# One-core hybrid decoder layer on Trainium2: low parts of expert 1's gate weights on VectorE, slot words fixed later, row tiles of one expert kept in the 64-slot tiles

## The chip, the core and the metric

The kernel runs on one core of one Trainium2 chip. The metric is the device time of one execution in microseconds, as the median of several runs. The profiles come from one execution each; times in them count from the start of the span.

The engines are called TensorE (PE in the profile, its weight loads PEld), VectorE (DVE), ScalarE (ACT), GpSimd (POOL) and SyncE (SP). In this kernel SP issues the loads of weights and of the row tables; GpSimd issues all gathers and scatters that go by an index.

## What is computed

One decoder layer on 2048 tokens of width 1024 with 16 learned meta tokens ahead of them: a pooling mixer and a gated linear attention side by side, an output projection, a routed mixture of 16 small SwiGLU experts, and a last norm. The part that matters here is the mixture:

```python
def hier_moe(x, w_rg, b_rg, w_re, b_re, w_gate, w_up, w_down):
    # g_logits, e_logits: x times two small matrices, plus biases
    g_prob = jax.nn.softmax(g_logits, axis=-1)
    g_sel = jnp.argmax(g_logits, axis=-1)                    # one of 4 groups
    e_prob = jax.nn.softmax(e_logits, axis=-1)               # of the 4 experts of that group
    top_p, top_i = lax.top_k(e_prob, TOP_K_IN_GROUP)         # the best two
    top_p = top_p / jnp.sum(top_p, axis=-1, keepdims=True)
    weights = p_g * top_p
    for e in range(N_EXPERTS):
        h = jax.nn.silu(xt @ w_gate[e]) * (xt @ w_up[e])     # 1024 -> 256
        y = y + combine[:, e:e + 1] * (h @ w_down[e])        # 256 -> 1024
```

Each token so has two experts of one group. Everything is float32.

## The kernel before, in words

**Split products.** A float32 product is made of three TensorE matmuls on rounded halves: high by high, low by high, high by low. `split` (L109 to L112) makes the halves of a tile: ScalarE writes the high part (L111), and VectorE, or the engine that is handed in, subtracts it from the tile for the low part (L112). `split_scaled` (L107, L108) does the same with a scale, for token rows that come out of a transpose.

**Slots.** The program does not compute all experts on all tokens. Routing gives each (token, expert) pair a slot, and each expert works on its slots: three row tiles j = 0, 1, 2 of 128, 128 and 64 slots (`rows`), 320 in all, for the experts at the first ten places, and two tiles (256 slots) for the places from `LARGE` = 10 on. Experts 0 and 1 have fixed places; the other fourteen are ranked by their token counts in `rank_experts` (L708), and `expert_at` then tells which expert's weights and table rows a place takes. Below, "expert e" means the one at place e.

**Routing, tile by tile.** Sixteen tiles of 128 tokens go through `out_proj`, `route_pick` (L579: logits, best group, best two experts, A = the two picks of each token as zeros and ones) and `route_rest` (L619). In `route_rest` TensorE multiplies A with a triangular matrix (`before_b`, L645) and the sum of all earlier tiles' A with ones (L647); the result says how many tokens ahead of each have the same expert, and VectorE makes slot numbers of it (L662 to L676) and a row of words for each pair (`rec`). GpSimd scatters these rows to a table in DRAM (L690), two scatters a tile. For the last tile (`t == NT`) two more matmuls make the total counts (L641, L642), which stand ahead of the picks, and VectorE adds them (L643); `rank_experts` reads them.

**Row tables and words.** `load_places` (L1105) reads the table back by SP: places 0 and 1 in one load, then 14 loads for a place each. A row has the token number (word 0, for the gather of its tokens), the weight (word 3), and others; words 1 and 2 say where a finished row is scattered or gathered, and `fix_words` (L1107 to L1121, seven VectorE instructions) works them out for a range of places.

**Around the end of routing.** Experts 0 and 1 start on the tokens of the early tiles before routing has ended: their tiles 0 and 2 are gathered early, and `gate_rows` (L984; matmuls L995 to L997) runs their gate and up products with the tokens as the stationary side, one accumulator for each tile. Tile 1 of each, the late rows, follows when the table is complete (`first_rows`). The order of these steps on an engine is that of the program, moved by the scheduler and by `must_follow`, which puts one instruction behind others on its engine: the last picks follow step k = 2 of the third group of `gate_rows` (`gate_ops[2]`, L1138).

**Weights.** Weight chunks of 128 x 1024 come in the order of `stream`: 0 to 3 expert 0's gate and up chunks, 4 to 7 expert 1's, 8 and 9 expert 0's down chunks, and so on. `load_chunks` (L747, issue L759) puts each in a tile of the pool `raw` of three buffers; `split_chunk` (L767) makes its halves. Expert 1's four chunks take their low parts from GpSimd (L1140); each frees a `raw` buffer, and SP then issues the load of the next chunk. SP works in order.

**The expert loop.** For expert e, `gate_up` (L963; matmuls L975 to L977; for experts 0 and 1 `gate_rows`) makes the hidden rows; `down` (L1020) multiplies them with the down weights (L1036 to L1041), and ScalarE evacuates the result with the slot's weight (L1052) into the expert's row tiles `RT[e]`. The rows are added to those of the token's other expert by indexed adds between `oe` and the row tile (L924); when e + 1 is under way, `square`, `finish` and `scale_out` (L1072, L1078) norm them and GpSimd scatters them to the output (L924, `out_dram`). Between the matmuls of `gate_up`, the function `between` puts the next expert's transposes (L946), weight splits and weight loads. The tiles of the tokens are `XG` (of the pool `xg`, and the two 64-slot tiles xs0 and xs1, `short`, in turn for j = 2). Row tiles `RT[e]` come from a pool `xr` of `RB` = 6 buffers, taken in turn (L1024), so one waits until the rows in its buffer have been scattered to the output.

Of the kernel before, what the change touches and what calls it, by code (L numbers as in the profile page):

```python
# [12 lines left out]
OP = mybir.AluOpType  # L13
# [4 lines left out]
NT = 16  # L18
# [8 lines left out]
LARGE = 10  # L27
# [43 lines left out]
def body(ctx, tc, I, O):  # L71
    nc = tc.nc
    V = nc.vector
# [82 lines left out]
    iota16 = iota("iota16", 16, 1)  # L156
    FIXED = 2
# [15 lines left out]
    counts = sl.tile([128, 16], F32, name="counts")  # L173
    place = per.tile([128, 16], F32, name="place")
# [445 lines left out]
    def route_rest(t):  # L620
# [9 lines left out]
        if t == EARLY + 1:  # L630
            nc.tensor.matmul(pp[:, 1], ones_b, acc[i % 2], start=True, stop=True)
            early = pp[:, 1]
            V.tensor_copy(counts, early)
            for row, at in ((late1, 128.0), (late2, float(SMALL)), (late3, float(CAP))):
                V.tensor_scalar(row[:, FIXED:], early[:, FIXED:], -1.0, at, op0=OP.mult, op1=OP.add)
            V.tensor_scalar(late2[:, :FIXED], early[:, :FIXED], -1.0, float(CAP), op0=OP.mult, op1=OP.add)
            V.tensor_scalar(late2[:, :FIXED], late2[:, :FIXED], 128.0, None, op0=OP.min)
            V.tensor_copy(late3[:, :FIXED], late2[:, :FIXED])
            V.scalar_tensor_tensor(late0[:, FIXED:], early[:, FIXED:], 48.0, iota16[:, FIXED:], op0=OP.mult, op1=OP.add)
        elif t == NT:  # L640
            nc.tensor.matmul(pp[:, 1], ones_b, acc[i % 2], start=True, stop=False)  # L641
            nc.tensor.matmul(pp[:, 1], ones_b, A, start=False, stop=True)  # L642
            V.tensor_tensor(counts, pp[:, 1], counts, op=OP.add)  # L643
        pp = pp[:, 0]
        picked[0] = nc.tensor.matmul(pp, before_b, A, start=True, stop=(t == EARLY + 1))  # L645
        if t != EARLY + 1:
            nc.tensor.matmul(pp, ones_b, acc[i % 2], start=False, stop=True)  # L647
        ngm, eg, sg, nm1, p2, den, w = T("ngm", 1), T("eg", 4), T("sg", 1), T("nm1", 1), T("p2", 1), T("den", 1), T("w", 2)
        V.tensor_scalar(ngm, gm, -1.0, None, op0=OP.mult)
        nc.scalar.activation(eg, lg[:, 0:4], AF.Exp, bias=ngm, accum_out=sg)  # L650
# [253 lines left out]
    with ExitStack() as c2:  # L904
# [30 lines left out]
        def row_tile(own=False):  # L935
            return mk.tile([128, D], F32, name="xr", bufs=RB) if own else me.tile([128, D], F32, name="xg", bufs=GB - 2)
# [83 lines left out]
        def down(e, js=None):  # L1020
            js = js or JS[e]
            ahead = e >= NE - 2
            if e not in RT:
                RT[e] = [row_tile(True) for j in JS[e]]  # L1024
            tags = ("sp", "o", "ds", "tp", "zg", "m2") if e else ("mm", "mm", "ds", "m2", "ds", "m2")
            units = [(j, a, bank(tags[2 * j + a])) for j in js for a in range(2)]

# [107 lines left out]
            for k in range(KB):  # L1135
                transposes(0, k, (0, 2), added[0])
        early = [gate_rows(0, 0, "mm"), gate_rows(0, 2, "mm", lambda k: k < 6 or transposes(1, k - 6, (0, 2)))]
        must_follow(picked[0], [gate_ops[2]])  # L1138
        for k in range(4):
            split_chunk(nc.gpsimd)  # L1140
            load_chunks(min(8 + k, 10))
        for k in range(2, KB):
            transposes(1, k, (0, 2))
        load_places(0, FIXED, slice(0, FIXED))
        fix_words(0, FIXED, iota16)
        for e in range(FIXED, NE):
            load_places(e, e + 1, expert(e))
        first_rows = [ind(XG[e][1], hn_dram, col(e, 1, 0), False) for e in range(2)]
# [16 lines left out]
                    transposes(0, i, (1,))  # L1165

        early_1 = [gate_rows(1, 0, "sp"), gate_rows(1, 2, "o", early_rest)]
        down(0, (0, 2))
        for e in range(NE):
            def between(i):  # L1170
                if e + 1 < NE and i % 2 == 0:
                    for k in range(i, i + 2):
                        transposes(e + 1, k, None if e else (1,))
                if e == 0:
                    if i in (2, 6):
                        fix_words(*((2, 9) if i == 2 else (9, 16)), place)
                    if i == 0:
                        for op in load_chunks(10 + WRB, mk):
                            must_follow(op, first_rows)
# [170 lines left out]
```

## Time and profile before

| | |
|---|---|
| median of the runs (1121.91, 1123.40, 1123.54) | 1123.4 us |
| the profiled execution, its span | 1121.29 us, 1119.5 us |
| mean granted clock of TensorE | 0.982 |
| TensorE (PE) busy | 1055.8 us, 94% |
| TensorE weight loads (PEld) | 946.5 us, 85% |
| VectorE (DVE) | 779.8 us, 70% |
| ScalarE (ACT) | 565.7 us, 51% |
| GpSimd (POOL) | 313.8 us, 28% |

A row of a timeline gives the start in the span, the duration, engine, line, operation, output and inputs, and in brackets how long the engine had been idle and what ended that. A row of the waits gives an engine, its instruction and whom it waited for: the total, how often, and the longest. A row of the windows gives each engine's busy time in a stretch, the granted clock of TensorE as a share of full speed (its levels are 1.2 and 2.4 GHz), and how busy the DMA engines were.

### The profile page before, as it was taken

The numbers are of one execution on the slowest core, as the hardware profiler recorded it, in microseconds if no ns is written. First come the engines' busy times: TensorE is split into PE (matmuls) and PEld (weight loads), VectorE is DVE, ScalarE is ACT, GpSimd is POOL, SyncE is SP. The second block draws the span as 40 slices with busy tenths as digits, with TensorE's granted clock in tenths as the row PEclk, the third lists the DMA queues.
The fourth block names the chain that finished last, engine by engine and source line by source line (L and its number), as shares of the span: only waits on it lengthen the run. The fifth ranks groups of instructions, "written<-read, shape, count | busy, mean of one in ns | idle before, by whom it ended". The sixth has DMA issues, their size and how long they took to land. (4 is left out here: it accounts for less than half of the span.)

```text
span 1119.5 us, 19115 instructions
## 1 busy us (share of the span) xinstructions
PE 1055.8 (94%) x6614; PEld 946.5 (85%) x6614; DVE 779.8 (70%) x2649; ACT 565.7 (51%) x1192; POOL 313.8 (28%) x276
## 2 busy tenths in 40 slices
PE   7999999999999999999999998879999999989982
PEld 5888888888888889999999998558998899988861
DVE  6476666545555776878777788747787788867873
ACT  7545444334433643333333334337767777667741
POOL 2000000000000000121111105524677777776551
PEclk9999999999999999999999999989999999989996
DMA  8412332111121352533434344488888997889852
GB/s 279 166 66 76 107 101 90 62 57 48 67 85 57 115 196 67 170 142 120 145 124 151 114 153 160 132 235 237 221 248 230 242 264 214 231 256 311 255 152 74
DMA packets 64471, 174.09 MB, mean 156 GB/s; under 512 B 21012, under 2 KB 21317, under 8 KB 64368
## 3 DMA queue, kind: packets, MB, share of 16 engines
q1 hardware_dynamic: 36272, 105.72, 27.7%
q0 software_dynamic: 25504, 58.53, 20.0%
q10 hardware_dynamic: 2592, 8.55, 2.1%
q8 instruction: 54, 0.88, 0.3%
q14 instruction: 49, 0.40, 0.1%
HBM read 143.74 MB, written 57.74 MB: 180 GB/s over the span
## 5 line engine op out<-in xcount | busy, mean ns | idle before, releaser
L441 POOL DMA_DIRECT2D y_dram<-y x16 | 8.6, 541 | 391.2 <-DVE y L439 391.2
L924 POOL DMA_INDIRECT oe<-xr,tab x40 | 69.3, 1732 | 69.0 <-ACT xr L1052 57.3
L321 PE MATMUL mm<-wb,XL 128*128 128x512 f32 (+1 forms) x240 | 83.6, 348 | 0.0
L322 PE MATMUL mm<-wb,XH 128*128 128x512 f32 (+1 forms) x240 | 83.0, 346 | 0.0
L690 POOL DMA_INDIRECT table<-rec,ix x32 | 33.3, 1042 | 176.8 <-DVE tmp L703 85.4
L320 PE MATMUL mm<-wb,XH 128*128 128x512 f32 (+1 forms) x240 | 82.2, 342 | 0.0
L924 POOL DMA_INDIRECT xr<-oe,tab x39 | 75.4, 1932 | 17.8 <-issue 9.8
L523 PE MATMUL mm<-XL,ws 128*128 128x256 f32 (+1 forms) x256 | 73.0, 285 | 0.2 <-DVE XL L112 0.2
L522 PE MATMUL mm<-XH,ws 128*128 128x256 f32 (+1 forms) x256 | 73.0, 286 | 0.0
L524 PE MATMUL mm<-XH,ws 128*128 128x256 f32 (+1 forms) x256 | 72.2, 282 | 0.0
L111 ACT ACTIVATE XH<-xt 128x1024 fp32r<-128x1024 f32 x32 | 33.8, 1058 | 56.4 <-PE mm L524 36.0
L924 POOL DMA_INDIRECT out_dram<-xr,tab x39 | 55.6, 1426 | 20.8 <-DVE sr_y L60 7.4
L975 PE MATMUL mm<-xh,ws 128*128 128x320 f32 (+1 forms) x168 | 51.3, 306 | 0.0
L976 PE MATMUL mm<-xl,ws 128*128 128x320 f32 (+1 forms) x168 | 51.2, 305 | 0.0
L977 PE MATMUL mm<-xh,ws 128*128 128x320 f32 (+1 forms) x168 | 51.0, 304 | 0.0
L320 PE MATMUL mm<-ws,XH 128*128 128x512 f32 x112 | 47.4, 423 | 2.0 <-ACT XH L111 2.0
L321 PEld LDWEIGHTS mm<-wb,XL 128*128 128x128 f32 x240 | 45.4, 189 | 4.4
L1078 DVE SCALAR_TENSOR_TENSOR xr<-xr,sr_y,fw 128x1024 f32<-128x1024 f32 (+1 forms) x39 | 48.7, 1278 | 0.5
L320 PEld LDWEIGHTS mm<-wb,XH 128*128 128x128 f32 x240 | 45.1, 188 | 4.6
L322 PEld LDWEIGHTS mm<-wb,XH 128*128 128x128 f32 x240 | 45.1, 188 | 4.5
L523 PEld LDWEIGHTS mm<-XL,ws 128*128 128x128 f32 x256 | 48.1, 188 | 0.7 <-DVE XL L112 0.4
L524 PEld LDWEIGHTS mm<-XH,ws 128*128 128x128 f32 x256 | 48.4, 189 | 0.3 <-issue 0.2
(654 smaller groups left out, 3840.8 us busy)
## 6 DMA issues: line engine op xcount, KB each, us to landing
raw<-in_wgu_e_dram SPq DMA_DIRECT2D x42, 512.0 KB, 5.2
xt<-in_xT_dram SPq DMA_DIRECT2D x32, 512.0 KB, 3.5
xn<-in_xn_dram SPq DMA_DIRECT2D x32, 512.0 KB, 3.5
wr<-in_wgu_e_dram SPq DMA_DIRECT2D x22, 512.0 KB, 5.9
raw<-in_wd_e_dram SPq DMA_DIRECT2D x20, 512.0 KB, 5.6
hn_dram<-xn ACTq DMA_DIRECT2D x16, 512.0 KB, 3.3
oe<-xn POOLq DMA_DIRECT2D x16, 512.0 KB, 3.7
wr<-in_wd_e_dram SPq DMA_DIRECT2D x12, 512.0 KB, 5.8
```

Of the source, the lines that this page charges most:

```text
L111: return (nc.scalar.activation(hi, src, AF.Copy), (eng or V).tensor_tensor(lo, src, hi.bitcast(F32), op=OP.subtract))
L320: nc.tensor.matmul(q, xh[:, k, :], wh[:, c0:c1_], start=(k == 0), stop=False)
L321: nc.tensor.matmul(q, xl[:, k, :], wh[:, c0:c1_], start=False, stop=False)
L322: nc.tensor.matmul(q, xh[:, k, :], wl[:, c0:c1_], start=False, stop=(k == KB - 1))
L522: nc.tensor.matmul(ps[:, b], WS[k][0][:, c], XH[:, k, o:], start=(k == 0), stop=False)
L523: nc.tensor.matmul(ps[:, b], WS[k][0][:, c], XL[:, k, o:], start=False, stop=False)
L524: nc.tensor.matmul(ps[:, b], WS[k][1][:, c], XH[:, k, o:], start=False, stop=(k == KB - 1))
L924: return nc.gpsimd.indirect_dma_start(out=out_, out_offset=off if scatter else None, in_=in_, in_offset=None if scatter else off, bounds_c ...
L975: nc.tensor.matmul(p[:, c0:c1_], wh, xh, start=(k == 0), stop=False)
L976: nc.tensor.matmul(p[:, c0:c1_], wh, xl, start=False, stop=False)
L977: nc.tensor.matmul(p[:, c0:c1_], wl, xh, start=False, stop=(k == KB - 1))
L1078: V.scalar_tensor_tensor(x[:n], x[:n], r[:n], fw[:n], op0=OP.mult, op1=OP.mult)
```

## The change

It has six edits.

1. In `route_rest` of the last tile the two matmuls of the totals, and VectorE's addition, stand behind the two matmuls of the picks instead of ahead of them.
2. The last picks follow step k = 6 of that group of `gate_rows` instead of step 2.
3. The low parts of expert 1's four weight chunks are made by VectorE instead of GpSimd; they follow `routed`, the last tile's cast of slot numbers.
4. `fix_words` for places 0 and 1 stands behind expert 1's early `gate_rows` instead of ahead of the 14 loads of single places.
5. `fix_words` for places 2 to 8 and 9 to 15 stand in expert 1's `between` instead of expert 0's.
6. Expert 10, the first with 256 slots, takes xs0 and xs1 as its row tiles instead of two of the pool `xr`. The buffers of the pool that it had (those of expert 8's tiles 0 and 1) go to expert 11, those of expert 11 to expert 12, and so on.

```diff
--- before.py
+++ after.py
@@ -637,14 +637,14 @@
             V.tensor_scalar(late2[:, :FIXED], late2[:, :FIXED], 128.0, None, op0=OP.min)
             V.tensor_copy(late3[:, :FIXED], late2[:, :FIXED])
             V.scalar_tensor_tensor(late0[:, FIXED:], early[:, FIXED:], 48.0, iota16[:, FIXED:], op0=OP.mult, op1=OP.add)
-        elif t == NT:
-            nc.tensor.matmul(pp[:, 1], ones_b, acc[i % 2], start=True, stop=False)
-            nc.tensor.matmul(pp[:, 1], ones_b, A, start=False, stop=True)
-            V.tensor_tensor(counts, pp[:, 1], counts, op=OP.add)
-        pp = pp[:, 0]
+        total, pp = pp[:, 1], pp[:, 0]
         picked[0] = nc.tensor.matmul(pp, before_b, A, start=True, stop=(t == EARLY + 1))
         if t != EARLY + 1:
             nc.tensor.matmul(pp, ones_b, acc[i % 2], start=False, stop=True)
+        if t == NT:
+            nc.tensor.matmul(total, ones_b, acc[i % 2], start=True, stop=False)
+            nc.tensor.matmul(total, ones_b, A, start=False, stop=True)
+            V.tensor_tensor(counts, total, counts, op=OP.add)
         ngm, eg, sg, nm1, p2, den, w = T("ngm", 1), T("eg", 4), T("sg", 1), T("nm1", 1), T("p2", 1), T("den", 1), T("w", 2)
         V.tensor_scalar(ngm, gm, -1.0, None, op0=OP.mult)
         nc.scalar.activation(eg, lg[:, 0:4], AF.Exp, bias=ngm, accum_out=sg)
@@ -1021,7 +1021,7 @@
             js = js or JS[e]
             ahead = e >= NE - 2
             if e not in RT:
-                RT[e] = [row_tile(True) for j in JS[e]]
+                RT[e] = short if e == LARGE else [row_tile(True) for j in JS[e]]
             tags = ("sp", "o", "ds", "tp", "zg", "m2") if e else ("mm", "mm", "ds", "m2", "ds", "m2")
             units = [(j, a, bank(tags[2 * j + a])) for j in js for a in range(2)]
 
@@ -1135,14 +1135,13 @@
             for k in range(KB):
                 transposes(0, k, (0, 2), added[0])
         early = [gate_rows(0, 0, "mm"), gate_rows(0, 2, "mm", lambda k: k < 6 or transposes(1, k - 6, (0, 2)))]
-        must_follow(picked[0], [gate_ops[2]])
+        must_follow(picked[0], [gate_ops[6]])
         for k in range(4):
-            split_chunk(nc.gpsimd)
+            must_follow(split_chunk()[1], [routed])
             load_chunks(min(8 + k, 10))
         for k in range(2, KB):
             transposes(1, k, (0, 2))
         load_places(0, FIXED, slice(0, FIXED))
-        fix_words(0, FIXED, iota16)
         for e in range(FIXED, NE):
             load_places(e, e + 1, expert(e))
         first_rows = [ind(XG[e][1], hn_dram, col(e, 1, 0), False) for e in range(2)]
@@ -1165,15 +1164,16 @@
                     transposes(0, i, (1,))
 
         early_1 = [gate_rows(1, 0, "sp"), gate_rows(1, 2, "o", early_rest)]
+        fix_words(0, FIXED, iota16)
         down(0, (0, 2))
         for e in range(NE):
             def between(i):
                 if e + 1 < NE and i % 2 == 0:
                     for k in range(i, i + 2):
                         transposes(e + 1, k, None if e else (1,))
+                if e == 1 and i in (2, 6):
+                    fix_words(*((2, 9) if i == 2 else (9, 16)), place)
                 if e == 0:
-                    if i in (2, 6):
-                        fix_words(*((2, 9) if i == 2 else (9, 16)), place)
                     if i == 0:
                         for op in load_chunks(10 + WRB, mk):
                             must_follow(op, first_rows)
```

The line numbers of the changed kernel are shifted a little: its picks are L641 and L643, its totals L645 and L646.

On TensorE, the last tile's picks and totals stood in expert 0's group of 64 rows in this way before (`mm` is the accumulator of `gate_rows`, `ws` and `xh`, `xl` its weights and tokens; `A` the picks, `acc` the sum of earlier tiles; the row with - is gone from this place):

```order
 L997 MATMUL mm<-ws_79,xh_8620 64x512
-L642 LDWEIGHTS ones_b
-L642 MATMUL m_8533<-A,ones_b 128x16
 L995 MATMUL mm<-ws_80,xh_8620 64x512
 L996 MATMUL mm<-ws_80,xl_8621 64x512
 L997 MATMUL mm<-ws_81,xh_8620 64x512
-L645 LDWEIGHTS before_b
-L645 MATMUL m_8533<-A,before_b 128x16
-L647 LDWEIGHTS ones_b
-L647 MATMUL m_8533<-acc_188,ones_b 128x16
 L995 MATMUL mm<-ws_80,xh_8620 64x512
```

and now in this way:

```order
 L997 MATMUL mm<-ws_85,xh_8620 64x512
+L641 LDWEIGHTS before_b
+L641 MATMUL m_8533<-A,before_b 128x16
+L643 LDWEIGHTS ones_b
+L643 MATMUL m_8533<-acc_188,ones_b 128x16
+L645 LDWEIGHTS ones_b
+L645 MATMUL m_8533<-acc_188,ones_b 128x16
+L646 LDWEIGHTS ones_b
+L646 MATMUL m_8533<-A,ones_b 128x16
 L946 MATMUL zg<-ident,xs_8627 128x128
```

The picks moved four steps further on, and the totals, which stood ahead of them and one of them in the first group of 128 rows, are now behind.

On VectorE, behind the last tile's routing, the changed kernel has this (`raw` and `wb` are a weight chunk and its halves, L722 to L725 the end of the ranking, `tp` and `zg` transposed tokens):

```order
L722 TENSOR_TENSOR sq<-sq,iota_114 128x196
L703 SCALAR_TENSOR_TENSOR tmp,sv_all<-E,lev 128x16
L112 TENSOR_TENSOR wb_87<-raw,wb_86 128x1024
L724 TENSOR_REDUCE t_8604<-sq 128x14
L112 TENSOR_TENSOR wb_89<-raw,wb_88 128x1024
L725 CAST expert_at<-t_8604 128x14
L112 TENSOR_TENSOR wb_91<-raw,wb_90 128x1024
L108 SCALAR_TENSOR_TENSOR wb_99<-tp,vecs,wb_98 128x192
L108 SCALAR_TENSOR_TENSOR wb_101<-zg,vecs,wb_100 128x192
```

Of expert 1's low parts the first three stand among the last steps of the ranking; the fourth follows a few rows on. Before, there was none of the four here.

The words of places 2 to 8 (L1115, 128x336) stood here on VectorE before (`HB` are the halves of hidden rows, `xl_8621` low halves of expert 0's tokens, eight of 128x128 for its late rows):

```order
L112 TENSOR_TENSOR HB<-zg,HB 128x2x128
L1004 TENSOR_TENSOR h<-mm,h 64x256
L112 TENSOR_TENSOR HB<-tp,HB 128x2x64
L1115 TENSOR_TENSOR sq<-tab,iota_114 128x336
L108 SCALAR_TENSOR_TENSOR xl_8621<-zg,vecs,xh_8620 128x128
L108 SCALAR_TENSOR_TENSOR xl_8621<-tp,vecs,xh_8620 128x128
L1116 TENSOR_TENSOR sq<-sq,place 128x336
```

and now here:

```order
L112 TENSOR_TENSOR HB<-zg,HB 128x2x128
L1004 TENSOR_TENSOR h<-mm,h 64x256
L108 SCALAR_TENSOR_TENSOR xl_8621<-zg,vecs,xh_8620 128x128
L112 TENSOR_TENSOR HB<-tp,HB 128x2x64
L108 SCALAR_TENSOR_TENSOR xl_8621<-zg,vecs,xh_8620 128x128
L108 SCALAR_TENSOR_TENSOR xl_8621<-tp,vecs,xh_8620 128x128
L1115 TENSOR_TENSOR sq<-tab,iota_114 128x336
L108 SCALAR_TENSOR_TENSOR xl_8621<-zg,vecs,xh_8620 128x128
L1116 TENSOR_TENSOR sq<-sq,place 128x336
```

They are behind three of the eight low halves, where they were ahead of all eight.

## Rows read from the trace of the kernel before

**Rows 1.** Windows: start:end, length; PE, PEld, DVE, ACT, POOL busy; clock, DMA share, GB/s.

```profile
695.00:744.80 49.80, 36.15 (x157) 24.55 (x156) 31.75 (x137) 17.66 (x38) 21.75 (x16) 0.86 0.54 167
709.70:713.20 3.50, 3.50 (x10) 1.85 (x9) 3.50 (x20) 0.74 (x2) 1.52 (x1) 0.51 0.02 5
735.30:740.30 5.00, 4.96 (x14) 3.27 (x15) 2.94 (x11) 1.66 (x5) 0.00 (x0) 0.50 0.64 201
982.10:1007.31 25.21, 21.25 (x138) 19.82 (x137) 16.54 (x34) 15.26 (x27) 17.37 (x13) 0.86 0.83 261
1007.31:1028.04 20.73, 19.64 (x143) 18.00 (x141) 18.21 (x36) 16.26 (x29) 14.15 (x8) 1.00 0.92 286
```

**Rows 2.** Waits from 695 to 745, those of TensorE.

```profile
PE zg L946 <- DVE xl L108: 7.0, 1, 7.0
...
PE m L641 <- DVE tmp L668: 2.7, 1, 2.7
PE m L642 <- DVE A L615: 2.7, 1, 2.7
```

**Rows 3.** Timeline of GpSimd, end of routing.

```profile
695.47 7.08 POOL L112 TENSOR_TENSOR wb<-raw,wb 128x1024 fp32r<-128x1024 f32 x3 [6.59 <-PE ds L572]
...
708.84 2.38 POOL L112 TENSOR_TENSOR wb<-raw,wb 128x1024 fp32r<-128x1024 f32 x1 [1.83 <-ACT wb L111]
714.03 1.03 POOL L690 DMA_INDIRECT table<-rec,ix  x1 [2.81 <-DVE sq L721]
715.36 1.76 POOL L690 DMA_INDIRECT table<-rec,ix  x1 [0.30 <-DVE t L724]
```

**Rows 4.** Timeline of VectorE, end of routing and the words of places 2 to 8.

```profile
696.61 1.32 DVE L663 TENSOR_TENSOR v<-v,late 128x16 f32<-128x16 f32 x1
...
700.23 2.35 DVE L667 TENSOR_TENSOR t<-lev,late_step 128x16 f32<-128x16 f32 x1
...
711.23 0.16 DVE L662 TENSOR_TENSOR v<-m,per_slot 128x16 f32<-128x16 f32 x1
...
713.58 0.16 DVE L676 CAST ix<-vv 128x2 int32<-128x2 f32 x1
...
715.04 1.22 DVE L112 TENSOR_TENSOR wb<-raw,wb 128x1024 fp32r<-128x1024 f32 x1
...
734.51 0.51 DVE L1115 TENSOR_TENSOR sq<-tab,iota 128x336 f32<-128x336 f32 x1 [7.33 <-DMA tab<-table]
```

**Rows 5.** Timeline of TensorE: the picks, and matmuls at either level of the clock.

```profile
709.42 0.18 PE L645 MATMUL m<-A,before_b 128*128 128x16 bf16 x1
...
711.83 0.63 PE L995 MATMUL mm<-ws,xh 128*64 128x512 f32 x1
712.26 0.63 PE L996 MATMUL mm<-ws,xl 128*64 128x512 f32 x1
...
714.53 0.39 PE L996 MATMUL mm<-ws,xl 128*64 128x512 f32 x1
714.76 0.40 PE L997 MATMUL mm<-ws,xh 128*64 128x512 f32 x1
```

**Rows 6.** Timeline of SP's queue: chunk loads, then the 15 table loads.

```profile
700.22 2.68 SPq L759 DMA_DIRECT2D raw<-in_wd_e_dram  x2
718.34 17.05 SPq L1105 DMA_DIRECT2D tab<-table  x15
```

**Rows 7.** DMA issues at 726.6 to 727.1 (place 8's table load) and 982.6 to 982.7.

```profile
tab<-table SPq DMA_DIRECT2D x1, 12.0 KB, 8.0
...
out_dram<-xr,tab POOLq DMA_INDIRECT x1, 7.4
```

**Rows 8.** Timelines of ScalarE, TensorE and ScalarE at experts 10 and 11.

```profile
990.14 0.69 ACT L1052 ACTIVATE xr<-sp,tab 128x512 f32<-128x512 f32 x1 [4.24 <-DMA out_dram<-xr,tab]
...
994.68 0.69 PE L946 MATMUL tp<-ident,xg 128*128 128x128 f32 x2 [3.96 <-ACT xr L1052]
...
1009.28 1.06 ACT L111 ACTIVATE ws<-raw 128x1024 fp32r<-128x1024 f32 x1 [2.24 <-DMA raw<-in_wgu_e_dram]
```

## The prediction

> **What bounds the kernel now.** The page's first two parts say TensorE (94% busy), so time can only come from TensorE's gaps and from stretches in which its clock is down. I read the windows view for the stretch in which routing ends and the first two experts start, then who ended TensorE's waits there, then the timelines of the engines named, then the same for experts 10 and 11. To see: from 695.00 to 744.80 TensorE is busy for 36.15 of 49.80 us, 13.65 idle, and at the lower of its two levels in two pieces, 3.50 us at 0.51 and 5.00 us at 0.50 [rows 1]. Against full speed these cost 3.50 x 0.49 = 1.7 and 5.00 x 0.50 = 2.5. Three waits make 12.4 of the 13.65: 2.7 and 2.7 on the routing of the last tile, 7.0 on a low half of expert 0's late rows [rows 2]. Later, the stretch between the down projections of experts 10 and 11 takes 25.21 us, the next one, with the same work, 20.73 [rows 1].
>
> **Change, part by part. Low parts off GpSimd.** GpSimd makes four low parts in 7.08 + 2.38 = 9.46 us [rows 3]. Each time, a tiny VectorE instruction beside them stretches and ends with them: three in a row of 1.32 to 2.35 us, 5.5 us together where 0.16 is usual (first and last of the three in [rows 4]). These are routing steps that TensorE's 2.7 + 2.7 hang on, so both waits go: the delay is longer than either. The clock's first dip, behind the second wait, goes too.
>
> **Picks later, totals behind them.** No matmul is added: the same four tiny ones. Without the two waits the picks of 709.42 [rows 5] would come at 704.0; the new place is four steps of three matmuls further on, 12 x 0.23 = 2.8 (spacing of full-clock matmuls, [rows 5]), so 706.8. The words for the last scatter need 713.58 - 711.23 = 2.35 from there, plus the cast [rows 4]: 709.3 instead of 713.7. The totals now stand behind the picks, and nobody but the ranking reads them.
>
> **Low parts on VectorE.** Each costs 1.22 [rows 4], 4.9 in all, on an engine that is at 31.75 of 49.80 in this stretch [rows 1]; they wait for routing's last cast and share VectorE with the ranking: ends at about 711.35, 712.8, 714.0, 715.3. This is a new wait, and three things queue behind it. TensorE has the rest of expert 0's early rows done at 708.9 and waits 2.45 for the first, some 0.7 for later ones, and 0.2 for the rest. SP: its last three chunk loads follow a low part each (before: GpSimd's, [rows 6]) and stand ahead of the row tables in SP's queue; the third leaves at 714.1. Last scatters: 709.75 and 711.1.
>
> **Row tables.** Before, the first load left at 718.34, 1.2 after the last scatter had ended (715.36 + 1.76) [rows 3, 6]. Now the scatters allow 711.1 + 1.03 + 1.2 = 713.3, and SP gets there at 714.5: 3.85 earlier. A scatter took 1.03, and 1.76 beside a low part on VectorE [rows 3, 4]: if both stretch, 1.46 more, most of it hidden behind SP's third chunk load. The Trainium skill (SBUF — State Buffer, "Who interferes with whom") has it that a VectorE instruction with two SBUF inputs contends only with a GpSimd instruction that reads SBUF; I read the issue of a scatter as none, so by it the price is 0. By the row it is up to 0.73 a scatter, and the sum is the same by both, since the chunk load hides it; only my lower bound takes the row's price.
>
> **Words of places 2 to 8.** VectorE holds the first one until the load of place 8 has landed: issued at 726.8, 8.0 us to landing, and the instruction starts at 734.51 [rows 4, 7]. These words are needed only for expert 2 onwards, but the instruction stands in VectorE's order ahead of low halves of expert 0's late rows, which TensorE needs. The change moves it from expert 0's part of the program to expert 1's, but the order rows show that VectorE runs it behind three of those eight halves, not behind all. So the wait stays, with its end 3.85 earlier: 730.7. TensorE, from 711.35, does what took it from 715.0 to 728.3 without its 1.2 of waiting, 12.1, plus 0.7, plus about 3.4 for three more transposes and the matmuls between them that may now go first: 727.6. It stalls until 731.3, 3.7 us, and has less left behind the stall. Then the second clock dip comes as before (2.5). The words of places 0 and 1 move with nothing behind them: their scatters come only with expert 1's down projection.
>
> **Stage sum.** Idle 13.65 becomes 2.45 + 0.7 + 0.2 + 3.7 = 7.05, gain 6.6; the first dip is gone, 1.7; the second stays. **8.3 us.** Bounds: with the words landed in time the 3.7 and its dip go too, 14.5; with both scatters stretched and landing late (table load at 716.9, 2.4 later) and one more dip (2.0) it is 3.9.
>
> **Expert 10's rows in the 64-slot tiles.** Before, its first evacuation waits 4.24 us for an output scatter (7.4 us to landing, issued at 982.6) which holds the row tile it takes over, and TensorE then waits 3.96 at its next transpose, and its clock goes down [rows 1, 7, 8]. The 64-slot tiles have had their last reader, expert 9's transposes, long before. Experts 11 to 13 take over buffers freed an expert earlier than before. So the stretch falls to the next one's pace: 25.21 - 20.73 = **4.5**. Upper bound 25.21 - 19.64 (TensorE's own work there) = 5.6. Lower bound 0: the DMA share is already 0.83, then 0.92, in these stretches, and a chunk's high part waits 2.24 for its load at 1009.28 [rows 1, 8]: an expert that runs earlier meets its weights later. I take 4.5, as the following stretch has that pace at that load.
>
> **Sum.** 8.3 + 4.5 = 12.8. The profiled execution is 1121.29 (span 1119.5): 1108.5. The median of the runs is 1123.4, 2.1 above it: **1110.6**. Costed at nothing: the moved totals (three tiny matmuls behind the picks, under VectorE's 2.35), and the words' instructions, the same number as before; without the wait that covers them, the fourteen of places 2 to 15 would be some 4 us of VectorE in expert 1's stretch, which has that idle.
>
> **Rivals.**
> - Late weights take over from expert 10's wait: the stage gains 8.3, the experts 0.5: 1123.4 - 8.8 = 1114.6. For it: 1009.28 and the DMA share. Against: the next stretch holds 20.73 under the same load.
> - Words in time: the loads of places 2 to 8 land 3.7 earlier still, since their 8.0 us come from a crowded stretch. Gain 14.5 + 4.5 = 19.0: 1104.4. Against: place 8's load leaves 8.4 after the first [rows 6, 7], so at 722.9, and would have to land in 4.7 instead of 8.0 to be there before TensorE, and the crowd goes forward with it.
> - The change does not do what it says: if VectorE got to the third low part only at 717.9, the table load would be where it was; the first two waits would come back as a wait on low parts, and with late weights as above it ends at 1121 to 1123. Against: VectorE's work before it ends at 709.3.
> - **Slower:** TensorE's clock. The new wait for low parts at 709 and those behind them are several short gaps in a row where there was one. If the clock stays at the lower level from there to the end of expert 0's late rows, each 512-column matmul comes 0.43 instead of 0.23 after the one before [rows 5], 0.20 more. Some 88 matmuls make 17.6: 1123.4 - 12.8 + 17.6 = 1128.2. It decides from 12.8 / 0.20 = 64 matmuls on. For it: both long idle times of this stretch are followed by the lower level. Against: it was over after 3.50 and 5.00 us [rows 1]. The Trainium skill (TensorE: Matmul & The Clock Gate, "What's actually happening") calls the throttled state the default, released by activity: by it short gaps with work between them need not bring it on.
>
> **How the numbers follow.** Under 0.2% (2.2 us) a measurement of this kernel cannot be told from no change. Forecast 0.57 (its own range 1107 to 1114); late weights 0.16; words in time 0.11; some of several parts lost, 1115 to 1120, 0.04; no effect 0.05; slower by the clock 0.07. The range reaches from the words in time with a little of the bound above (1103) to below the point where parts are lost (1118). Faster 0.88, same 0.05, slower 0.07.
>
> **What would show it.** Right: no wait on the routing ahead of the picks; first table load near 714.5; TensorE's stall on a low half of late rows about 3.7 long, ended by the words of places 2 to 8; the matmuls of expert 0's late rows begun some 8 us earlier; no evacuation of expert 10 waiting for an output scatter; its stretch near 20.7. Wrong: the first table load still near 718; a stall of 7 that only moved; the stretch of expert 10 over 24, with a chunk's high part waiting for its load; a granted clock near 0.5 through the whole of expert 1's early rows.

## The result, and the profile after

The changed kernel takes 1109.15 us (median of 4 runs, 1107.33 to 1110.83), beside 1123.47 of the kernel before on the same chip: a ratio of 0.9874, 95% interval 0.9852 to 0.9896, or 14.2 us (11.7 to 16.6) less. 1110.6 was predicted. Run again on another occasion, the same kernel gave 0.9868 (0.9848 to 0.9889). The profiled execution took 1107.88 us, its span is 1106.2, 13.3 shorter than before.

Where the 13.3 come from is read off at fixed places of the program. At the picks of the first full routing tile (454.40 before, 453.51 after) the changed kernel is 0.9 ahead, and 1.0 at the picks of tile 15 (695.71, 694.74): nothing of the change has run by then, so this is no gain of it. From those picks to expert 2's down projection it takes 83.4 us where it took 93.7: **10.3**. From expert 10's down projection to the end 135.4 instead of 137.4: **2.0**. Between the two, both take the same.

The windows that answer to [rows 1]: the stretch from 0.7 us ahead of tile 15's picks to the first matmul of expert 0's late rows, the two dips of the clock in it, and the stretches of experts 10, 11 and 12 (start:end, length, busy time of PE, PEld, DVE, ACT, POOL, granted clock, DMA share, GB/s):

```profile
694.03:734.17 40.14, 34.37 (x158) 23.52 (x156) 27.31 (x138) 17.85 (x37) 11.40 (x12) 0.93 0.52 146
711.50:714.90 3.40, 3.40 (x11) 2.00 (x10) 2.16 (x7) 0.76 (x1) 0.00 (x0) 0.51 0.87 265
731.90:735.40 3.50, 3.50 (x12) 2.49 (x11) 2.42 (x10) 3.10 (x7) 1.63 (x1) 0.52 0.68 223
970.80:989.71 18.91, 18.91 (x139) 17.48 (x138) 16.01 (x34) 15.23 (x27) 15.86 (x11) 1.00 0.96 307
989.71:1011.00 21.29, 19.54 (x143) 18.01 (x141) 18.70 (x36) 15.93 (x28) 17.28 (x11) 1.00 1.00 316
1011.00:1033.38 22.38, 20.46 (x139) 19.02 (x137) 16.04 (x32) 14.49 (x26) 12.86 (x9) 0.92 0.97 292
```

TensorE is idle 40.14 - 34.37 = 5.77 us in the first stretch, where it was 13.65. Both dips are still there, 3.40 and 3.50 long instead of 3.50 and 5.00 (before, the clock was down in the last 5 us of the stall ahead of the second dip as well: 730.35 to 735.30 reads 0.50). Expert 10's stretch is 18.91 instead of 25.21, with TensorE busy throughout; those of experts 11 and 12 are longer than before (20.73, 20.60).

The waits of TensorE in the first stretch, as in [rows 2]:

```profile
PE zg L946 <- DVE xl L108: 3.5, 1, 3.5
PE sp L997 <- DVE wb L112: 2.2, 1, 2.2
```

Both waits on routing are gone, the stall of 7.0 is 3.5, and there is a new one of 2.2 on the first low part. SP's queue and VectorE's, as in [rows 4, 6]:

```profile
711.85 1.55 SPq L759 DMA_DIRECT2D raw<-in_wd_e_dram  x2
714.44 15.96 SPq L1105 DMA_DIRECT2D tab<-table  x15
```

```profile
695.63 0.18 DVE L663 TENSOR_TENSOR v<-v,late 128x16 f32<-128x16 f32 x1
...
709.15 1.22 DVE L112 TENSOR_TENSOR wb<-raw,wb 128x1024 fp32r<-128x1024 f32 x1
...
730.09 0.51 DVE L1115 TENSOR_TENSOR sq<-tab,iota 128x336 f32<-128x336 f32 x1 [3.86 <-DMA tab<-table]
```

The routing step that took 1.32 beside GpSimd's low parts takes 0.18. Since this trace is 1.0 ahead from the start, the predicted times are compared from tile 15's picks on: the first table load leaves 19.7 us behind them (18.8 predicted), the words of places 2 to 8 start 35.3 behind (35.0 predicted). The first matmul of expert 0's late rows comes 39.4 behind them, 9.7 earlier than before (some 8 predicted).

In the stretches of experts 11 and 12, ScalarE and TensorE show this:

```profile
995.99 1.06 ACT L1072 ACTIVATE sq<-xs 128x1024 bf16<-128x1024 f32 x1 [1.93 <-DMA xs<-oe,tab]
...
1015.77 1.06 ACT L111 ACTIVATE wb<-wr 128x1024 fp32r<-128x1024 f32 x1 [3.27 <-DMA wr<-in_wd_e_dram]
```

```profile
999.50 0.44 PE L946 MATMUL tp<-ident,xg 128*128 128x128 f32 x2 [1.75 <-ACT xr L1052]
```

ScalarE stands for 1.93 us at the square of expert 10's second tile, whose indexed add into xs has not landed; behind it in its order are expert 11's evacuations, for which TensorE waits 1.75. At 1015.77 it stands for 3.27 us at the high part of a down chunk, ahead of expert 12's evacuations, and TensorE waits 1.92 for them. This second wait is not new; the kernel before has it at the same place, and TensorE waited 1.32 for it:

```profile
1032.14 1.06 ACT L111 ACTIVATE wb<-wr 128x1024 fp32r<-128x1024 f32 x1 [2.83 <-DMA wr<-in_wd_e_dram]
```

### The profile page after: what moved, and what is told of

It reads as the page before. It is cut to its first block, busy times and chain, and to the rows that moved or that the text cites. A ratio compares the mean times of both kernels' runs of the same rounds, so it can differ in the third digit from the quotient of the medians.

```text
span 1106.2 us, 19107 instructions
## 1 busy us (share of the span) xinstructions
PE 1052.7 (95%) x6614; PEld 945.6 (85%) x6614; DVE 777.1 (70%) x2653; ACT 565.3 (51%) x1192; POOL 309.8 (28%) x272
## 5 line engine op out<-in xcount | busy, mean ns | idle before, releaser
L924 POOL DMA_INDIRECT oe<-xr,tab x38 | 65.5, 1723 | 68.1 <-ACT xr L1052 56.3
L924 POOL DMA_INDIRECT out_dram<-xr,tab x37 | 50.5, 1365 | 22.4 <-DVE sr_y L60 9.3
L112 DVE TENSOR_TENSOR wb<-raw,wb 128x1024 fp32r<-128x1024 f32 x39 | 47.6, 1221 | 9.1 <-ACT wb L111 9.1
```

What stands on the lines that cost most here:

```text
L112: (eng or V).tensor_tensor(lo, src, hi.bitcast(F32), op=OP.subtract))
L924: return nc.gpsimd.indirect_dma_start(out=out_, out_offset=off if scatter else None, in_=in_, in_offset=None if scatter else off, bounds_c ...
```

## The experiments

Two questions were open: which edit carries the stage of the first experts, and why edit 6 gave 6.3 us in its own stretch but only 2.0 to the end. All ratios are to the kernel before, run beside the kernel in question.

**Edit 6 taken back.**

```diff
-                RT[e] = short if e == LARGE else [row_tile(True) for j in JS[e]]
+                RT[e] = [row_tile(True) for j in JS[e]]
```

Expected: 

> The changed kernel without edit 6: expert 10 takes its row tiles from the pool xr again. Theory A (edit 6 removes the wait, but the weights then arrive too late, since the DMA share is already 0.96 to 1.00 in these stretches): the stretch from expert 10's to expert 11's down projection is back at 25 us with a 4 us wait for an output scatter, the later stretches are back at 20.5 to 20.7 and 22.3; net 2 us slower than the changed kernel, about 1111. Theory B (as the prediction had it: 4.5 are kept, and the slower stretches of experts 11 to 14 come from something else): later stretches stay at 21.3, 22.4, 24.1 while expert 10's is back at 25; 4.5 to 6.3 slower, 1113.5 to 1115.5.

Measured: 0.9926 (0.9905 to 0.9947). Expert 10's stretch is 25.29, the next three 21.10, 21.02 and 20.37; from expert 10 on it takes 138.0 us, 137.4 in the kernel before.

**Edit 6 alone, on the kernel before.** Expected: 

> The kernel before with edit 6 alone. Theory A: the stretch of expert 10 falls from 25.2 to about 19, the ones of experts 11 to 14 grow by 4 together; the kernel before less 2, about 1121.4. Theory B: 4.5 to 6.3 less, 1117 to 1119. Nothing changes ahead of expert 10 by either.

Measured: 0.9958 (0.9941 to 0.9975), 4.7 us less (2.8 to 6.6). The stretches of experts 10 to 13 are 18.91, 21.46, 22.24 and 19.99, as in the changed kernel. The times lie at theory B's figures in both: 0.9926 is 1115.2 on the first scale (theory A 1111, theory B 1113.5 to 1115.5), and theory A's 2 us for edit 6 alone are outside the interval of the 4.7. The stretches go with theory A: the one of expert 11 is 21.3 to 23.1 in all eight traces with edit 6 and the squares where they were, 20.7 and 21.1 in the two without it, so part of the 6.3 is given back. Neither theory holds whole. In the same traces expert 10 to the end takes 133.7 to 135.4 with edit 6, 137.4 and 138.0 without it (the kernel without the output scatters of three experts, below, is left aside). The net gain is some 3 by the traces, and that lies within the interval of the runs, 2.8 to 6.6. The other five edits together, which is what the first of these two kernels has, gain 8.3 us (6.0 to 10.7).

**Words of places 2 to 8 further back.**

```diff
-            V.tensor_tensor(eq, w[:, :, :, 5:6].to_broadcast(full), iota16[:, None, None, :].to_broadcast(full), op=OP.is_equal)
+            first_op = V.tensor_tensor(eq, w[:, :, :, 5:6].to_broadcast(full), iota16[:, None, None, :].to_broadcast(full), op=OP.is_equal)
+            if lo == FIXED:
+                must_follow(first_op, hidden_done)
```

Expected: 

> The changed kernel, with the words of places 2 to 8 held on VectorE behind the hidden rows of expert 0's late rows. Theory A (TensorE's 3.5 us stall at 727 to 731 and the dip of the clock behind it, 1.6, come from these words alone): no stall there, 5 us faster than the changed kernel, about 1104, and 5 earlier at the down projection of expert 2. Theory B (something else is late next, a weight chunk of expert 0 or 1 or the late rows' gather): the stall moves to another instruction and the time is within 2 of the changed kernel.

**Words where they were, edits 4 and 5 taken back.** Expected: 

> The changed kernel without edits 4 and 5: the words stand where they stood in the kernel before. Theory A (three low halves ahead of the words let TensorE work on for some 3.4 us before the stall): the words' first instruction still starts near 730, but TensorE stalls some 3 us longer, about 1112. Theory B (their place in the program makes no difference, the table loads being earlier is all): same as the changed kernel, 1109.

Measured: 0.9876 (0.9854 to 0.9898) with the words further back, 0.9865 (0.9843 to 0.9888) with them where they were. Both are the changed kernel's time within the intervals: theory B in both, and **edits 4 and 5 have no effect that these runs can tell**. What came in place of the words shows in the trace with the words further back (ScalarE's timeline):

```profile
730.77 0.37 ACT L107 ACTIVATE xh<-zg,vecs 128x128 fp32r<-128x128 f32 x1 [3.51 <-remote]
```

ScalarE stands for 3.51 us ahead of the high part of the first late transpose, which TensorE had started at 727.57, and TensorE waits 2.35 for what follows. What ended ScalarE's wait is not in the trace ("remote" is a release that the trace can't name), and the traces of this group of runs hold no landings of DMAs. Edit 6 taken back and edits 4 and 5 taken back show a wait of 3.45 and 3.23 there too.

**The changed kernel once more**, without an edit. Expected: 

> The changed kernel once more, beside the three below. 0.985 to 0.99 of the kernel before, as measured first. In the stage from the picks of the fifteenth tile to the down projection of expert 2 it takes 83.4 us; if ScalarE's unexplained wait of 3.3 us ahead of expert 0's late rows (seen in the four runs above) comes here as well, TensorE's stall there is ended by ScalarE and not by the words of places 2 to 8.

Measured: 0.9868. ScalarE's wait is not there, and its stage is 81.4 us. TensorE's waits:

```profile
PE sp L997 <- DVE wb L112: 2.2, 1, 2.2
PE zg L946 <- DVE xl L108: 1.3, 1, 1.3
```

So even with the same program the stall on low halves is 1.3 here and 3.5 in the first trace. ScalarE's wait belongs to the occasion, its cause stays open, and the experiment on the words was made where it hid them: whether they would cost something without it was not tried again.

**Low parts back on GpSimd, picks still late (edit 3 taken back).**

```diff
-            must_follow(split_chunk()[1], [routed])
+            split_chunk(nc.gpsimd)
```

Expected: 

> The changed kernel with the four low parts of expert 1 back on GpSimd (edit 3 undone, the picks stay late). Theory A (GpSimd's low parts stretch the tiny routing instructions on VectorE, and that is what held the picks): VectorE's instructions beside them take 1.3 to 2.4 us again, the last picks wait for A until about 708 in the first trace's count, first table load 2.5 to 4 later, 3 to 6 us slower than the changed kernel. Theory B (the wait for low parts on VectorE, 2.2 us, costs as much as the stretching did, and placing the picks later is what gained): within 2 us of the changed kernel.

Measured: 0.9945 (0.9924 to 0.9967), some 8.6 us slower than the changed kernel in the same group of runs. The chain as theory A had it is there, in VectorE's timeline and TensorE's:

```profile
699.64 2.35 DVE L665 TENSOR_TENSOR t<-t,step 128x16 f32<-128x16 f32 x1
```

```profile
710.44 0.17 PE L641 MATMUL m<-A,before_b 128*128 128x16 bf16 x1 [2.06 <-DVE A L615]
```

A routing step takes 2.35 again, and the last picks wait for A. The loss is larger than theory A's 3 to 6, nearly the whole gain of the stage, which is 92.5 us here. What is left, 0.9945, cannot be told from edit 6 alone (0.9958): **without edit 3 the edits 1, 2, 4 and 5 gain nothing that these runs can tell**. Edit 3 without edits 1 and 2 was not run.

**Low parts on GpSimd, but behind the routing.**

```diff
-            must_follow(split_chunk()[1], [routed])
+            must_follow(split_chunk(nc.gpsimd)[1], [routed])
```

Expected: 

> The changed kernel with the four low parts on GpSimd again, but behind the last tile's cast of slot numbers, as VectorE has them now. Theory A (what GpSimd's low parts cost is the routing instructions that stretch beside them): no stretched routing step, last picks as early as in the changed kernel; but each low part takes 2.4 instead of 1.2, so the fourth ends 5 us later and the first table load leaves some 2 to 4 later: 2 to 5 us slower than the changed kernel, still 4 to 7 faster than with low parts on GpSimd ahead of the routing. Theory B (stretching costs nothing, what matters is on which engine the low parts are): as slow as with GpSimd's low parts early, 0.9945 of the kernel before.

Measured: 0.9939 (0.9919 to 0.9960), theory B by the time. The trace (GpSimd, SP, TensorE):

```profile
710.97 9.45 POOL L112 TENSOR_TENSOR wb<-raw,wb 128x1024 fp32r<-128x1024 f32 x4
```

```profile
715.69 2.66 SPq L759 DMA_DIRECT2D raw<-in_wd_e_dram  x2
718.63 15.87 SPq L1105 DMA_DIRECT2D tab<-table  x15
```

```profile
713.39 0.80 PE L997 MATMUL sp<-wb,wb 128*128 128x512 f32 x1 [2.80 <-POOL wb L112]
```

No routing step is stretched and the picks come as early as in the changed kernel (10.82 us after tile 15's in both). But four low parts take 9.45 us where VectorE takes 1.22 each, SP's chunk loads follow them, and the table load leaves at 718.63 instead of 714.44. The stage is 92.5 us. So half of theory A holds (no stretching), and its time does not. But the time is lost at another place than with low parts ahead of the routing: expert 0's late rows begin 40.0 us after tile 15's picks, nearly as early as in the changed kernel (39.4), and the 9 us are lost behind them. There SP's next weight loads, which stand behind the row tables in its queue, leave at 736.06 instead of 731.82, and the first takes 11.0 us to landing instead of 5.2. ScalarE stands 3.77 us for it, and TensorE stalls at expert 2's transposes:

```profile
747.09 1.06 ACT L111 ACTIVATE ws<-raw 128x1024 fp32r<-128x1024 f32 x1 [3.77 <-DMA raw<-in_wgu_e_dram]
```

```profile
754.56 0.47 PE L946 MATMUL zg<-ident,xs 128*128 128x128 f32 x1 [5.43 <-DVE xl L108]
```

**One low part on GpSimd, three on VectorE.** The edit above, for the first chunk only and without the `must_follow`. Expected: 

> The changed kernel with the first of expert 1's four low parts on GpSimd and three on VectorE. Theory A (TensorE's wait of 2.2 us for the first low part and the dip of the clock behind it are the price of edit 3): that wait goes, one or two routing steps stretch by 1 to 2 us where the picks have 3 us of slack, 2 to 4 us faster than the changed kernel. Theory B (the table loads or the gathers set when the late rows begin, whatever happens here): TensorE waits the same time later, within 1.5 us of the changed kernel.

Measured: 0.9894 (0.9867 to 0.9920), not faster. The wait of 2.2 on a low part is gone, and a wait of 2.91 for a low half of tokens (L108) has come, which on VectorE stands behind the three low parts in a row; later TensorE stalls 3.80. The ratio is 0.0026 above that of the changed kernel beside it, with intervals that overlap. The wait only changed its name.

The traces of the stage side by side, in us counted from tile 15's picks:

| kernel | first table load | first matmul of expert 0's late rows | expert 2's down projection |
|---|---|---|---|
| before; edit 6 alone | 22.6, 22.6 | 49.1, 49.9 | 93.7, 94.6 |
| low parts on GpSimd early | 23.2 | 48.0 | 92.5 |
| low parts on GpSimd late | 24.0 | 40.0 | 92.5 |
| changed, twice | 19.7, 19.5 | 39.4, 36.4 | 83.4, 81.4 |
| edit 6 back; words further back; words back | 19.6, 19.5, 19.4 | 40.1, 40.8, 40.9 | 83.7, 85.6, 84.4 |
| one low part on GpSimd | 19.4 | 42.2 | 86.6 |
| the four kernels below, this stage unchanged | 19.5 | 36.6 to 41.1 | 81.0 to 84.6 |

**Without the output scatters of three experts.** The rows of experts 9, 10 and 11 are left out of the output.

```diff
-            store(e, j, x)
+            if e not in (9, 10, 11):
+                store(e, j, x)
```

Expected: 

> The changed kernel without the output scatters of experts 9, 10 and 11 (their rows of the output are left out), which takes 1 MB or more from the DMA engines in each of the stretches of experts 10 to 12. Theory A (the weights for experts 11 to 14 come late because the DMA engines are full once expert 10 runs faster): high parts no longer wait 3.3 us for a chunk near expert 12, the stretches of experts 11 and 12 fall from 21.3 and 22.4 to about 20, 3 to 5 us faster. Theory B (the waits come from the order of evacuations, squares and high parts on ScalarE, not from transfers): these stretches stay within 0.5.

Measured: 0.9834 (0.9807 to 0.9861), less than the changed kernel beside it, though the two profiled spans agree (1105.8, 1106.0). Expert 11's stretch grew to 24.03 (22.99 in the changed kernel run beside it), expert 12's is 19.31 (20.22); experts 10 to 13 together take 82.44 and 82.99. So neither theory's stretches came. The DMA share fell from 0.99 to 0.90 in expert 11's stretch, and its length did not follow: fewer transfers did not shorten it. ScalarE waits 3.45 for the add into xs there, and TensorE 3.42 behind it.

**Squares of expert 10 behind expert 11's down projection.**

```diff
-            if e > 1:
+            late_square = e == LARGE + 1
+            if e > 1 and not late_square:
                 for j in JS[e - 1]:
                     square(e - 1, j)
...
             down(e, None if e else (1,))
+            if late_square:
+                for j in JS[e - 1]:
+                    square(e - 1, j)
```

Expected: 

> The changed kernel with the squares of expert 10's rows behind expert 11's down projection in the program instead of ahead of it. Theory A (the stretch of expert 11 is long, 21.3 to 23, because ScalarE, in order, waits 2 us for the indexed add into xs1 ahead of expert 11's evacuations): TensorE's wait of 1.7 on an evacuation goes, that stretch falls to about 20, 1 to 3 us faster than the changed kernel. Theory B (the wait for late weights behind it takes its place, a slot later): the stretch falls, the next one grows by as much, same time within 1.

**The same for experts 10 to 12** (`late_square = LARGE < e < NE - 2`). Expected: 

> The same for the squares of experts 10 to 12. Theory A: the stretches of experts 11 to 13 all near 20, 2 to 4 us faster than the changed kernel. Theory B: as much is lost further on (later output scatters, a longer tail), same time within 1.

Measured: 0.9814 (0.9792 to 0.9835) and **0.9801 (0.9777 to 0.9824)**, medians 1101.84 and 1101.33 us: both beat both kernels (the changed kernel was not run beside them; its 0.9848 to 0.9889 lies apart from both intervals). The stretches of experts 10 to 13 in the second:

```profile
971.93:990.86 18.93, 18.93 (x139) 17.48 (x137) 16.03 (x34) 15.23 (x27) 15.88 (x11) 1.00 0.97 308
990.86:1011.25 20.39, 19.83 (x142) 18.00 (x141) 18.21 (x36) 15.48 (x27) 15.59 (x11) 1.00 1.03 320
1011.25:1029.87 18.62, 18.62 (x138) 17.53 (x137) 15.10 (x33) 15.78 (x29) 11.52 (x7) 1.00 1.04 364
1029.87:1048.53 18.66, 18.66 (x138) 17.56 (x137) 15.31 (x33) 14.70 (x26) 10.45 (x7) 1.00 0.96 295
```

TensorE is busy throughout in three of them, at 308, 364 and 295 GB/s, where 292 to 316 went with the long ones. ScalarE reaches the square late enough that it waits 0.54 instead of 2, with two of the four evacuations already done:

```profile
995.12 0.69 ACT L1052 ACTIVATE xr<-sp,tab 128x512 f32<-128x512 f32 x1
995.69 0.70 ACT L1052 ACTIVATE xr<-o,tab 128x512 f32<-128x512 f32 x1
996.93 1.06 ACT L1072 ACTIVATE sq<-xs 128x1024 bf16<-128x1024 f32 x1 [0.54 <-DMA xs<-oe,tab]
```

The times are theory A's, and more than it expected; its path is not shown by the first of the two. There the square, behind the same two evacuations, still waits:

```profile
995.85 1.06 ACT L1072 ACTIVATE sq<-xs 128x1024 bf16<-128x1024 f32 x1 [1.85 <-DMA xs<-oe,tab]
...
1015.29 0.67 ACT L1052 ACTIVATE xr<-sp,tab 128x512 f32<-128x512 f32 x1
...
1017.93 1.08 ACT L111 ACTIVATE wb<-wr 128x1024 fp32r<-128x1024 f32 x1
```

TensorE waits 1.65 behind it, and expert 11's stretch is 21.86, between the 21.29 and 22.99 of the changed kernel. What fell is expert 12's:

```profile
988.46:1010.32 21.86, 19.87 (x143) 18.03 (x142) 18.35 (x36) 16.20 (x29) 17.06 (x11) 1.00 0.99 304
1010.32:1029.04 18.72, 18.72 (x138) 17.57 (x137) 16.91 (x35) 15.25 (x27) 13.57 (x8) 1.00 1.03 354
```

With the squares moved, another instruction changed its place in ScalarE's order: the high part of the down chunk, which waits 3.27 us ahead of expert 12's evacuations in the changed kernel (1015.77), now runs behind them (1017.93). The load itself is no faster, 7.7 us from issue to landing and 7.9 in the changed kernel; it is only asked for later.

**Late squares without edit 6.** Expected: 

> The changed kernel with the late squares of experts 10 to 12, but without edit 6 (expert 10's row tiles from the pool xr). Theory A (the wait of the squares for an indexed add is what edit 6 was paid back with): without edit 6 these squares hardly wait, so the late squares gain 1 or less here; expert 10's stretch is back at 25, those of experts 11 to 13 are 20.5 to 21; about 0.992 of the kernel before, 12 to 14 us slower than with edit 6 and late squares. Theory B (late squares gain by themselves, with edit 6 or without): stretches of 11 to 13 fall to 20.4, 18.6, 18.7, only expert 10's is 25; about 0.986 of the kernel before, 5 to 7 slower than with edit 6.

Measured: 0.9855 (0.9829 to 0.9881). The time lies at theory B's figure, and two of three stretches do as well (21.02, 18.61, 18.65 behind 25.26): the late squares gain with or without edit 6. Here, too, the high part of that chunk runs behind the evacuations. Experts 12 and 13 together take 37.3 us with late squares, with edit 6 or without, and 41.1 to 42.3 in the changed kernel, the kernel before and the one with edit 6 taken back; expert 11's stretch, where the square waits, is 21.86 and 20.39 in the two traces with late squares and edit 6 (21.29 and 22.99 in the changed kernel's two), and without edit 6 stays at 21.0. So by the traces most of the gain comes where the chunk's high part changed its place; that place was not varied by itself. The four stretches of experts 10 to 13 together:

| | squares ahead | squares behind |
|---|---|---|
| without edit 6 | 87.0, 87.8 | 83.5 |
| with edit 6 | 82.5, 83.0, 82.6 | 76.6 |

Edit 6 is worth 4 to 5 us with the squares ahead and 6.9 with them behind.

## Why the prediction was right, and where not

The time and its sign were right (12.8 forecast, 14.2 measured), and the likeliest case was the one that came. In the traces its two terms are both off, in opposite directions, and as far as they cancel the total is luck. The runs cannot tell either term from the forecast: all edits but 6 gain 8.3 us (6.0 to 10.7), with 8.3 forecast, and edit 6 alone 4.7 (2.8 to 6.6), with 4.5 forecast.

**The stage: 8.3 forecast, 10.3 in the trace.** Right: both routing waits went, counted from tile 15's picks the table load and the words came within 0.9 us of the times given, and the stall was 3.5 (3.7). The new wait on low parts is 2.2 (2.45). The 0.7 and 0.2 for further low parts did not come, so the idle time is 5.77 instead of 7.05. Wrong: "the first dip is gone". A dip of 3.40 us stands behind the new wait of 2.2; the second is shorter instead (3.50 of 5.00). The wait alone does not settle it: in nine traces TensorE waits the same 2.2 us there, and the clock falls behind it in five of them and stays up in four (edit 6 taken back, words further back, and both kernels with late squares and edit 6). The two dips together cost 3.40 x 0.49 + 3.50 x 0.48 = 3.4, before 4.2. That makes 7.9 + 0.8 = 8.7 by the stretch that was costed. The remaining 1.6 have no term in the sum; most of them lie behind the stretch, up to expert 2's down projection, and no experiment took them apart.

The working gave the routing waits most of the weight. Up to the late rows the traces go with it: with GpSimd's low parts ahead of the routing they begin at 48.0, with the same low parts behind it at 40.0, although the first table load is then the latest of all (24.0). The two kernels differ in one thing more there, the words of places 2 to 8 stand behind two of the eight low halves in the first and behind four in the second, so the share of the routing alone is not shown. Behind the late rows there is a price that the working did not meet, since VectorE's low parts are quick: slow ones behind the routing hold SP's chunk loads, the weight loads behind the row tables come late, and the 9 us are lost again. So both must hold, the routing free and SP not held. The part of SP's queue is read from the trace; it was not varied by itself.

**Words of places 2 to 8.** The stall of 3.7 came as forecast, but it was mistaken for a price. Taken away (words further back) it gained nothing, with another wait in its place, and in the second trace of the changed kernel the stall on low halves was 1.3.

**A scatter beside a low part.** The last scatter took 1.19 beside two of them; the one ahead of it, whose last 0.6 us ran beside the first, took 1.00 (GpSimd's timeline after):

```profile
708.73 1.00 POOL L690 DMA_INDIRECT table<-rec,ix  x1 [7.92 <-DVE sq L721]
710.04 1.19 POOL L690 DMA_INDIRECT table<-rec,ix  x1 [0.31 <-issue]
```

So 0.2, between the row's 0.73 and the 0 that followed from the Trainium skill (SBUF — State Buffer, "Who interferes with whom"), and nearer to the rule. The Trainium skill has it in the same section that a VectorE instruction with two SBUF inputs contends with a GpSimd instruction that reads SBUF; with low parts on GpSimd the trace agrees, 2.35 for a step of 0.17.

**Expert 10: 4.5 forecast; 6.3 in its stretch, 2.0 left at the end in this trace, some 3 over all of them, 4.7 in the runs of edit 6 alone.** The sum can stand, the way to it not. The step that failed is "the stretch falls to the next one's pace". It fell to 18.91, TensorE's own work there, below the 19.64 that was taken as its bound; and the next pace was no floor but was itself held by waits of ScalarE ahead of the evacuations. The rival of late weights saw that something would be given back, but the wait for a chunk that the prediction feared is there before the change as well (2.83, then 3.27), and it costs because of its place in ScalarE's order.

What the change adds, and the prediction did not look for, is a wait of the square: expert 10's stretch is 6.3 us shorter, but the indexed add into its second tile lands 25.1 us behind its down projection, where it was 23.7 (9.9 us from issue to landing instead of 6.6). ScalarE stands for it ahead of the next expert's evacuations, 1.7 to 2.3 us in the eight traces with edit 6 and the squares where they were, and not at all in the kernel before and in the one with edit 6 taken back. That this is what gives back the part lost in experts 11 to 13 is likely, not shown: the four stretches speak for it (with late squares edit 6 keeps 6.9 us there, from one trace each, with the squares ahead 4 to 5), the times of the runs do not tell it: the late squares gain some 7.5 us with edit 6 and 8.0 without, each from runs that were not made beside each other. What is given back from expert 14's down projection to the end (50.4 and 50.2 us without edit 6, 50.7 to 52.9 with it) has no cause shown.

**The rivals on the other side.** The clock did not stay low: it was down 3.40 and 3.50 us. The change did what it says.

## What to carry to other kernels

An instruction that waits for a late transfer and whose own result nobody needs soon belongs behind those in its engine's order that feed the bottleneck: here the squares of three experts, moved behind one down projection each, gained some 7.5 us (0.9868 to 0.9801, from two groups of runs), half as much as the whole change. Look at the whole order afterwards, though: by the traces most of this gain came where the high part of a weight chunk had changed its place along with them. When a wait is removed, look in the same stretch for what the consumer reaches earlier than its data, on the in-order engines first. And a stall read from one trace is a place to try, not a price: the one on the words was 7.0, 3.5 and 1.3 us, and moving it away gained nothing.

## What the runs showed that was not expected

- GpSimd takes 9.45 us for four subtractions of 128x1024, VectorE 1.22 for each; with GpSimd's four behind the routing, where no routing step is stretched, the stage was as long as with them ahead of it (92.5 both), and the time was lost at another place.
- ScalarE's waits of 3.2 to 5.3 us ahead of the late rows, in one group of four runs, with nothing in their traces that explains them; these traces hold no landings of DMAs. The only other trace without landings, late squares without edit 6, has a wait of 2.47 there.
- The DMA engines moved 364 GB/s at a share of 1.04 where 292 at 0.97 had looked full, and a stretch as short as that one (18.66 and 18.62) went with 295 at 0.96: neither the share nor the rate told how long a stretch was.
